# Keeping ScalarE's logarithm and exponential table loaded, and GLA's key·value products as three split fp32r passes

## The chip, the cores and the metric

The kernel runs on one core of one Trainium2 chip. The metric is the device time of one execution in microseconds, lower is better. A few executions are taken, and their median counts; one more execution is recorded by the profiler, and all rows below come from that one.

## The reference, cut to what matters

Two blocks work on 512 tokens of width 1024 in float32. The first block has two layers, one with latent attention, one with gated linear attention (GLA), each followed by a convolutional feed-forward layer. The second block runs differential attention beside a recurrent unit, gates the two branches, and ends in a mixture of 16 experts. The lines that the change touches:

```python
# GLA: 4 heads of 128 keys x 256 values, 8 chunks of 64 tokens
k_dec = k * jnp.exp(tot[:, :, None] - cum)
upd = jnp.einsum('bnchk,bnchv->nbhkv', k_dec, v)
def step(state, inp):
    g, u, qc = inp
    state = state * g[..., None] + u
    return state, jnp.einsum('bchk,bhkv->bchv', qc, state)
...
# second block
o = rms_norm_2(o, attn_subln_gain[l]) * (1.0 - lam_init)     # 8 heads
g_attn, g_lru = jnp.split(jax.nn.sigmoid(gate_pre + b_gates[l]), 2, axis=-1)
merged = g_attn * attn_d + g_lru * lru_d
x = x + jnp.einsum('bsd,de->bse', merged, w_out[l])
h2 = rms_norm_2(x, norm2_gain[l])
x = x + hierarchical_moe(h2, ...)                            # top 2 of one group of 4 experts
```

## The kernel before

All large products are made in a split form: an fp32 operand is divided into a high part (`ACT` copy into an fp32r tile, L286) and a low part (`DVE` subtract, L287), and `mm3` issues high·high, high·low and low·high (L309 to L311). Weights arrive by DMA on SP's queue as raw fp32 and are split in the same way by L94 (ACT) and L95 (DVE). PSUM has rings of banks, called "mm" for the linears and "at" for the rest.

**GLA** (`gla`). For each pair of heads the generator `recurrence` runs over eight chunks of 64 tokens beside the linears of the layer, one `step` between two pieces of a linear. `update(n)` multiplies the chunk's decayed keys, transposed (`kdt`, 64 tokens on the partitions by 128 keys), with the values (`v`, 64 tokens by 256 columns) for the two heads into one bank, L924: 32 such matmuls in all, in plain fp32. DVE adds the result to the running state (L929). L939 multiplies the queries with the state, also in fp32, one head into the upper and one into the lower 64 partitions of the result. `kdt` is a plain fp32 copy by DVE (L905 transposes), `v` one by ACT from the four banks of the value linear.

**Table loads.** ScalarE evaluates functions from a table set, and another set is brought in by an ACT_TABLE_LOAD. `rstd` (1/sqrt by exp of a logarithm) issues Ln at L366 and Exp at L367, and DVE finishes with a Newton step (L368 to L370). `log_exp_table` (L374) loads the set that holds both at a few places. Around rstd the kernel uses Tanh for gates (L1402, and L1454 for those kept "late") and Sqrt in the recurrent unit. A scheduler orders each engine's instructions; nothing but data ties Ln and Exp to the preload.

**Sub-norm stage** (second block, after attention). `sub_norm` brings eight heads back (L1279), squares (L1280), sums by PE, takes rstd, scales with DVE (L1284) and splits (L286, L287) into the inputs of the output linear. Gate linears (L1402) run beside it, and the late gates are held as plain sums until L1454 takes their Tanh.

**Routing stage** (`out_and_route`). For each of four token tiles and two halves: the residual is added (L1536), transposed by PE (L1539), squared by ACT (L1542), scaled (L1547 by DVE, L1549 by ACT) and multiplied with the router's weights (L1551). Then rstd over the row sums gives `route_rs` (L366, L367, L370). `route(t)` on DVE finds the two experts of a token (L1647 to L1663, result `sel`), PE counts positions from `sel` (L1667, L1668), and L1719 makes one-hot rows. After the fourth tile L1728 builds the lists by which POOL gathers the tokens of the first experts (L1758), PE transposes those (L1767), and the experts start. L1568 scales the rows that the gather reads.

Of the kernel before, what the change touches and what calls it, by code (L numbers as in the profile page):

```python
# [16 lines left out]
AF = mybir.ActivationFunctionType  # L17
# [4 lines left out]
P = 128  # L22
# [133 lines left out]
class Kern:  # L156
    def __init__(self, tc, ctx, a):
        self.tc, self.nc, self.a = tc, tc.nc, a
        self.n = 0
        self.cp = ctx.enter_context(tc.tile_pool(name="const", bufs=1))  # L160
        self.sp = ctx.enter_context(tc.tile_pool(name="small", bufs=4))
        mem = ctx.enter_context(tc.tile_pool(name="mem", bufs=1))
        psp = ctx.enter_context(tc.tile_pool(name="psum", bufs=1, space=PSUM))
        def new(n, dt, b):
            t = mem.tile([P, n], dt, tag=b, name=b)
            self.tags[id(t)] = b, n
            return t
        self.tags = {}
        self.rawq = deque(new(RAWN, F32, f"raw{i}") for i in range(3))
        self.wp = {"w": deque((new(PIECE, F32R, f"wh{i}"), new(PIECE, F32R, f"wl{i}")) for i in range(5))}  # L170
        self.pool = {F32: deque(), F32R: deque()}
        self.home, self.parts, self.held = {}, {}, set()
        self.bigs = {F32: [], F32R: []}
        quads = [(F32, new(RAWN, F32, f"f{i}"), 4) for i in range(5)]
        self.quads = [t for _, t, _ in quads]
        rquads = [(F32R, new(RAWN, F32R, f"rq{i}"), 4) for i in range(4)]
        self.rquads = [t for _, t, _ in rquads]
        ones = [(F32R, new(S, F32R, f"r{i}"), 1) for i in range(21)]
        bigs = [(dt, new(2 * S, dt, f"b{j}{i}"), 2) for j, dt in enumerate((F32, F32R)) for i in range(2)]

        self.side = None
        self.mem = mem
        for dt, t, k in quads + rquads + ones + bigs:
            parts = self.parts[id(t)] = [t[:, i * S:(i + 1) * S] for i in range(k)]
            if k == 2:
                self.bigs[dt].append(t)
            for x in parts:
                self.pool[dt].append(x)
                self.home[id(x)] = dt
        self.quad_parts = {id(x) for t in self.rquads for x in self.parts[id(t)]}  # L190
        self.banks = [psp.tile([P, S], F32, tag=f"ps{i}", name=f"ps{i}") for i in range(8)]
        self.rings(mm=4, at=4)
# [170 lines left out]

    def rstd(self, y, t, v, eps):
        nc = self.nc
        nc.scalar.activation(t, v, AF.Ln, bias=self.eps[eps])  # L366
        nc.scalar.activation(y, t, AF.Exp, scale=-0.5)  # L367
        nc.vector.scalar_tensor_tensor(t, y, -0.5, y, ALU.mult, ALU.mult)  # L368
        nc.vector.scalar_tensor_tensor(t, v, eps, t, ALU.add, ALU.mult)
        nc.vector.scalar_tensor_tensor(y, t, 1.5, y, ALU.add, ALU.mult)  # L370


    def log_exp_table(self):
        self.tc.keep_in_program_order(self.nc.scalar.preload_act_table_set("natural_log_exp_and_others"))  # L374


    def rstd_small(self, y, v):
# [466 lines left out]
    def gla(self, w, xh, xl, r_dram, after):  # L844
        nc, a = self.nc, self.a
        x = xh, xl
        self.rings(mm=5, at=3)
        wa2 = self.F()
        nc.scalar.dma_start(wa2[:32], a["w_a2"])
        at = self.F()  # L850
# [29 lines left out]
        q, kdt = [None] * 4, [None] * 4  # L880

        def ev(m, ps, t0, t1):
            p, j = divmod(m, 4)
            h = 2 * p + j % 2
            if j < 2:
                q[h] = self.F()
                nc.scalar.activation(q[h], ps, AF.Copy, scale=float(128 ** -0.5))
            else:

                nc.vector.tensor_tensor(kd[h], kd[h], ps, ALU.mult)  # L890
                ps = self.ps("at")
                for t in range(4):
                    nc.tensor.transpose(ps[:, t * P:t * P + P], kd[h][:, t * P:t * P + P], self.ident)
                kdt[h] = self.F()
                nc.vector.tensor_copy(kdt[h], ps)
                self.free(kd[h])

        on = [None] * 8
# [14 lines left out]
        def recurrence(p, v):  # L913
            st, oc = self.Fs(2), None
            on[4 * p:4 * p + 4] = self.Fs(4)
            late = None

            def update(n):
                t, p0 = n // 2, 64 * (n % 2)
                pu = self.ps("at")  # L920
                for i in range(2):
                    h = 2 * p + i
                    hs = slice(i * 256, i * 256 + 256)
                    nc.tensor.matmul(pu[:, hs], kdt[h][p0:p0 + 64, t * P:t * P + P], v[t][p0:p0 + 64, hs], start=True, stop=True)  # L924
                    cur, prev = (st[i][:, j * 256:j * 256 + 256] for j in (n % 2, 1 - n % 2))
                    if n == 0:
                        nc.vector.tensor_copy(cur, pu[:, hs])
                    else:
                        nc.vector.scalar_tensor_tensor(cur, prev, dec[h][:, n:n + 1], pu[:, hs], ALU.mult, ALU.add)  # L929
            update(0)  # L930
            yield
            for n in range(8):
                if n < 7:
                    update(n + 1)
                t = n // 2
                po = self.ps("at")[:, :256]

# [8 lines left out]
                if n % 2:  # L946
# [7 lines left out]
                    for i in range(2):  # L954
                        o = oc[:, i * 256:i * 256 + 256]
                        nc.vector.tensor_scalar(o, o, mv[:, i, 0:1], rs[:, i:i + 1], ALU.subtract, ALU.mult)
                    late = lambda t=t, oc=oc: turned(p, t, oc)
                yield
            self.free(st, v, q[2 * p:2 * p + 2], kdt[2 * p:2 * p + 2])
            late()  # L960

        def step():
            next(rec, None)

        def values(w, then):
            v, pss = self.Fs(4), [self.ps() for _ in range(4)]
            for i in range(4):
                z = next(w)
                then.prime(1) if i == 3 else w.prime(1)
                for t, ps in enumerate(pss):  # L970
                    ts = slice(t * P, t * P + P)
                    self.mm3(ps, [(xh[2 * i + k][:, ts], xl[2 * i + k][:, ts], *z(k)) for k in range(2)], i == 0, i == 3)
                    if i == 3:
                        nc.scalar.activation(v[t], ps, AF.Copy)
                z.done()
                step()
            return v
# [26 lines left out]
        ps = self.ps()[:32]  # L1004
# [315 lines left out]
    def lru_tile(self, m, px, pg, raw, y_dram):  # L1320
# [35 lines left out]
            nc.vector.scalar_tensor_tensor(u, u, 1.0, x, ALU.add, ALU.mult)  # L1356
            au.append((r, u, q))
        self.free(xh, xl, gh, gl)
        nc.scalar.activation(vv, vv, AF.Sqrt, scale=0.25)
        for d in range(2):  # L1360
            r, u, q = au[d]
            nc.vector.tensor_tensor(u, u, vv[:, d], ALU.mult)
# [34 lines left out]
    def gate(self, wg, i, h, ring="mm", then=None, late=False):  # L1397
        w = next(wg)
        (then or wg).prime(1)
        ps = self.mtile(w, KD, h, ring=ring)  # L1400
        t = self.F()
        self.nc.scalar.activation(t, ps, AF.Identity if late else AF.Tanh, bias=self.half_bg[:, i:i + 1], scale=0.5)  # L1402
        return t

    def second_norm(self, x, h, t0, t1):
# [3 lines left out]
    def second_block(self, x, h, o_dram, y_dram, g_dram):  # L1409
# [41 lines left out]
        for _ in norm:  # L1451
            pass
        for t in late.values():
            nc.scalar.activation(t, t, AF.Tanh)  # L1454
        self.free(h)


# [594 lines left out]
```

## Time and profile before

| what | value |
| --- | --- |
| runs | 2389.17, 2392.74, 2393.77 us (median 2392.74) |
| profiled execution | 2387.63 us, span 2385.7 us |
| PE, DVE, ACT busy | 98%, 70%, 55% of the span |
| mean granted TensorE clock | 0.99 |
| ACT_TABLE_LOADs | 56 of 1283 ns |

PE is the busiest engine nearly everywhere: of the span of 2385.7 us it has no work on it for 58.4 us. The granted clock is given as a share of 2.4 GHz, so 0.50 in a row is the 1.2 GHz level.

### The profile page before, as it was taken

To read this page: it belongs to the slowest core of one execution; us is meant where nothing else is said; L and a number is where in the kernel's file an instruction comes from. 1 tells how busy PE (TensorE), PEld (TensorE's weight loads), DVE (VectorE), ACT (ScalarE), POOL (GpSimd) and SP (SyncE) were. 2 spreads that over 40 slices of the span, in tenths; PEclk is the share of its full clock that TensorE was granted. 3 is DMA by queue.
4 is the path that set the end of the run, shared out by engine and by line. 5 is a ranking of instruction groups with operands and counts; after the bars stand their busy time and mean duration, and the time that the engine had idled before them with its cause. 6 is when DMAs were issued, how large, how long until landed. Compare 5 with 4: busy or idle time off the path is not lost.

```text
span 2385.7 us, 31840 instructions
## 1 busy us (share of the span) xinstructions
PE 2327.3 (98%) x12188; PEld 1963.4 (82%) x12188; DVE 1672.1 (70%) x3241; ACT 1301.5 (55%) x2053; POOL 82.1 (3%) x78
## 2 busy tenths in 40 slices
PE   8999999999999999999999999999999999799997
PEld 6888888888889776888888898888888778688886
DVE  7867678555558646585555578888888664699986
ACT  5444445333336424353333366777777843678886
POOL 0000000000000000000000000000000000012211
PEclk9999999999999999999999999999999999799999
DMA  4622211222232323222222323222322346499995
GB/s 172 208 73 83 102 58 71 107 91 104 90 114 69 124 80 102 84 88 107 91 104 90 114 73 122 89 93 72 124 71 98 115 163 252 153 353 395 389 391 179
DMA packets 66683, 325.32 MB, mean 136 GB/s; under 512 B 8256, under 2 KB 8896, under 8 KB 38112
## 3 DMA queue, kind: packets, MB, share of 16 engines
q1 hardware_dynamic: 50544, 281.83, 31.9%
q0 software_dynamic: 7584, 26.22, 3.8%
q10 hardware_dynamic: 8400, 15.21, 2.1%
q8 instruction: 97, 1.59, 0.3%
q14 instruction: 58, 0.48, 0.1%
HBM read 295.44 MB, written 27.79 MB: 135 GB/s over the span
## 4 chain that ended last, share of the span: by engine, by line
PE 74%; issue 9%; ACT 6%; DMA 5%; DVE 4%; POOL 1%; POOLq 0%; ACTq 0%; DVEq 0%
PE ps L309 22%; PE ps L310 22%; PE ps L311 22%; DMA out<-b,s 3%; PE ps L924 1%; PE ps L721 1%; ACT wh L94 1%; POOL out L1847 1%; PE ps L405 1%; PE ps L1234 0%; PE ps L1203 0%; ACT L366 0%; PE ps L1254 0%; ACT f L1239 0%; PE ps L939 0%
## 5 line engine op out<-in xcount | busy, mean ns | idle before, releaser
L94 ACT ACTIVATE wh<-raw 128x1024 fp32r<-128x1024 f32 (+2 forms) x374 | 383.4, 1030 | 527.7 <-PE ps L310 442.1
L95 DVE TENSOR_TENSOR wl<-raw,wh 128x1024 fp32r<-128x1024 f32 (+2 forms) x374 | 440.8, 1186 | 207.3 <-ACT wh L94 200.7
L310 PE MATMUL ps<-r,wh 128*128 128x512 f32 (+1 forms) x1308 | 485.0, 371 | 0.0
L309 PE MATMUL ps<-rq,wh 128*128 128x512 f32 (+1 forms) x1216 | 453.6, 375 | 12.6 <-ACT rq L286 9.9
L311 PE MATMUL ps<-rq,wl 128*128 128x512 f32 (+1 forms) x1216 | 450.3, 372 | 0.0
L309 PE MATMUL ps<-r,wh 128*128 128x512 f32 (+1 forms) x1160 | 421.0, 364 | 1.1 <-ACT r L433 0.8
L311 PE MATMUL ps<-r,wl 128*128 128x512 f32 (+1 forms) x1160 | 421.3, 364 | 0.7 <-DVE wl L95 0.7
L310 PE MATMUL ps<-rq,wh 128*128 128x512 f32 (+1 forms) x1032 | 372.7, 362 | 1.8 <-DVE rq L287 1.3
L311 PE MATMUL ps<-wh,r 128*128 128x512 f32 (+1 forms) x928 | 318.0, 343 | 0.4 <-DVE r L287 0.4
L310 PEld LDWEIGHTS ps<-r,wh 128*128 128x128 f32 x1308 | 246.3, 188 | 43.2 <-issue 3.1
L309 PEld LDWEIGHTS ps<-rq,wh 128*128 128x128 f32 x1216 | 229.6, 190 | 56.5 <-ACT rq L286 10.8
L311 PEld LDWEIGHTS ps<-rq,wl 128*128 128x128 f32 x1216 | 229.5, 189 | 38.6 <-issue 0.5
L309 PEld LDWEIGHTS ps<-r,wh 128*128 128x128 f32 x1160 | 218.7, 189 | 36.2 <-ACT r L433 1.5
L311 PEld LDWEIGHTS ps<-r,wl 128*128 128x128 f32 x1160 | 219.2, 189 | 35.0 <-DVE wl L95 1.0
L309 PE MATMUL ps<-wh,r 128*128 128x512 f32 (+1 forms) x640 | 238.7, 373 | 0.0
L310 PE MATMUL ps<-wl,r 128*128 128x512 f32 (+1 forms) x640 | 234.6, 367 | 0.0
L310 PEld LDWEIGHTS ps<-rq,wh 128*128 128x128 f32 x1032 | 195.8, 190 | 33.2 <-DVE rq L287 2.4
L311 PEld LDWEIGHTS ps<-wh,r 128*128 128x128 f32 x928 | 176.6, 190 | 21.3 <-DVE r L287 0.8
L309 PEld LDWEIGHTS ps<-wh,r 128*128 128x128 f32 x640 | 121.6, 190 | 18.3 <-issue 0.4
L310 PEld LDWEIGHTS ps<-wl,r 128*128 128x128 f32 x640 | 121.7, 190 | 17.9 <-issue 0.3
L310 PE MATMUL ps<-wl,rq 128*128 128x256 f32 (+1 forms) x320 | 95.3, 298 | 1.5 <-DVE wl L95 1.5
L309 PE MATMUL ps<-wh,rq 128*128 128x256 f32 (+1 forms) x320 | 96.4, 301 | 0.0
(653 smaller groups left out, 3512.3 us busy)
## 6 DMA issues: line engine op xcount, KB each, us to landing
raw<-w_ffn_up SPq DMA_DIRECT2D x44, 1024.0 KB, 4.8
f<-w_exp_in SPq DMA_DIRECT2D x21, 1024.0 KB, 9.7
raw<-w_exp_in SPq DMA_DIRECT2D x18, 1024.0 KB, 9.8
raw<-w_ffn_dn SPq DMA_DIRECT2D x16, 1024.0 KB, 4.8
raw<-w_exp_dn SPq DMA_DIRECT2D x9, 1024.0 KB, 10.4
f<-w_exp_dn SPq DMA_DIRECT2D x9, 1024.0 KB, 9.0
raw<-w_gla SPq DMA_DIRECT2D x17, 512.0 KB, 3.3
raw<-w_mla_o SPq DMA_DIRECT2D x8, 1024.0 KB, 4.9
```

What stands on the lines that cost most here:

```text
L94: k.nc.scalar.activation(h, src, AF.Copy)
L95: k.nc.vector.tensor_tensor(l, src, h.bitcast(F32), ALU.subtract)
L309: self.nc.tensor.matmul(out, ah, bh, start=f, stop=False)
L310: self.nc.tensor.matmul(out, ah, bl, start=False, stop=False)
L311: self.nc.tensor.matmul(out, al, bh, start=False, stop=e)
L405: nc.tensor.matmul(ps, ones, s[:, :n], start=i == group - 1, stop=i == len(tiles) - 1)
L721: self.nc.tensor.transpose(ps[:, o + (j - i) * P:o + (j - i + 1) * P], ea[j][:, i * P:(i + 1) * P], self.ident)
L924: nc.tensor.matmul(pu[:, hs], kdt[h][p0:p0 + 64, t * P:t * P + P], v[t][p0:p0 + 64, hs], start=True, stop=True)
L1847: self.nc.gpsimd.indirect_dma_start(out=out, out_offset=bass.IndirectOffsetOnAxis(ap=idx, axis=0), in_=y, in_offset=None, bounds_check=S - ...
```

## The change

Two edits that do not touch each other.

**Function tables.** Ln and Exp of `rstd` are queued behind the latest preload of the common table. The preload itself is queued behind the functions of other tables that were noted before it (`others`: Sqrt of the recurrent unit, Tanh of gates that are not late, late Tanh). The late Tanhs are queued behind all Exps of rstd that were noted (`exps`). All of these are orders within one engine's queue, without a semaphore. ACT_TABLE_LOADs in the program go from 56 to 41.

**Products.** `products(t)` handles two chunks at once: `kdt` and `v` are split into high and low fp32r tiles, and for each head the three passes are issued, each for the first chunk (rows 0 to 63, into one bank) and then the second (rows 64 to 127, into another). That makes 12 matmuls for each of 8 calls, 96 in all, for 32 fp32 ones. `kdt` and `v` go back with the last products. The rings of banks become 4 and 4, from 5 and 3.

```diff
     def rstd(self, y, t, v, eps):
         nc = self.nc
-        nc.scalar.activation(t, v, AF.Ln, bias=self.eps[eps])
-        nc.scalar.activation(y, t, AF.Exp, scale=-0.5)
+        ln = nc.scalar.activation(t, v, AF.Ln, bias=self.eps[eps]).ins
+        ex = nc.scalar.activation(y, t, AF.Exp, scale=-0.5).ins
+        for i in (ln, ex):
+            self.queue_behind(i, [self.table])
+        self.exps.append(ex)
...
     def log_exp_table(self):
-        self.tc.keep_in_program_order(self.nc.scalar.preload_act_table_set("natural_log_exp_and_others"))
+        self.table = self.tc.keep_in_program_order(self.nc.scalar.preload_act_table_set("natural_log_exp_and_others"))
+        self.table = getattr(self.table, "ins", self.table)
+        self.queue_behind(self.table, self.others)
+        self.others, self.exps = [], []
...
-        self.rings(mm=5, at=3)
+        self.rings(mm=4, at=4)
...
-                kdt[h] = self.F()
-                nc.vector.tensor_copy(kdt[h], ps)
+                kdt[h] = self.split_new(ps)
...
-            def update(n):
-                t, p0 = n // 2, 64 * (n % 2)
-                pu = self.ps("at")
+            def products(t):
+                pus = self.ps("at"), self.ps("at")
+                ts = slice(t * P, t * P + P)
+                for i in range(2):
+                    hs = slice(i * 256, i * 256 + 256)
+                    (kh, kl), (vh, vl) = kdt[2 * p + i], v[t]
+                    for j, (ka, vb) in enumerate(((kh, vh), (kh, vl), (kl, vh))):
+                        for c, pu in enumerate(pus):
+                            rows = slice(c * 64, c * 64 + 64)
+                            nc.tensor.matmul(pu[:, hs], ka[rows, ts], vb[rows, hs], start=j == 0, stop=j == 2)
+                if t == 3:
+                    self.free(v, kdt[2 * p:2 * p + 2])
+                return pus
+
+            def update(n, pu):
...
-                    nc.tensor.matmul(pu[:, hs], kdt[h][p0:p0 + 64, t * P:t * P + P], v[t][p0:p0 + 64, hs], start=True, stop=True)
...
-                        nc.scalar.activation(v[t], ps, AF.Copy)
+                        v[t] = self.split_new(ps)
...
         for t in late.values():
-            nc.scalar.activation(t, t, AF.Tanh)
+            i = nc.scalar.activation(t, t, AF.Tanh).ins
+            self.queue_behind(i, self.exps)
+            self.others.append(i)
```

The order of PE's instructions where the first products stand, before: L924 is the fp32 product, the L309 to L311 rows are the linear that runs beside it.

```order
L311 MATMUL ps_118<-r_90,wl_79 128x512
L924 MATMUL ps_119<-f_82,f_81 128x256
L309 MATMUL ps_114<-rq_88,wh_72 128x512
L310 MATMUL ps_114<-r_91,wh_72 128x512
L311 MATMUL ps_114<-rq_88,wl_73 128x512
L924 MATMUL ps_119<-f_82,f_80 128x256
L309 MATMUL ps_114<-rq_87,wh_72 128x512
```

And of the change, where L941 is the new product, L310 to L312 the linear's passes:

```order
L312 MATMUL ps_115<-r_90,wl_79 128x512
L941 MATMUL ps_120<-r_109,r_98 128x256
L941 MATMUL ps_121<-r_109,r_98 128x256
L941 MATMUL ps_120<-rq_86,r_98 128x256
L941 MATMUL ps_121<-rq_86,r_98 128x256
...
L941 MATMUL ps_121<-r_109,r_102 128x256
L310 MATMUL ps_116<-rq_88,wh_72 128x512
```

Each head's single product stood between pieces of the linear; now twelve stand in one run, alternating between two banks.

ScalarE's queue at the second token tile of the routing stage, before (L1542 square, L1549 scaling for the router, L1568 scaling for the gather):

```order
L1542 ACTIVATE b_111,route_ss<-b_110 128x512
L1549 ACTIVATE f_84<-ps_119,par 128x128
L366 ACT_TABLE_LOAD
L366 ACTIVATE s_15570<-s_15569,eps_175 128x1
L367 ACT_TABLE_LOAD
L367 ACTIVATE route_rs<-s_15570 128x1
L1549 ACTIVATE f_84<-ps_119,par 128x128
```

and of the change, with the same lines at new numbers (L1574 for L1542, L1581 for L1549, L367 and L368 for Ln and Exp):

```order
L1574 ACTIVATE b_111,route_ss<-f_83 128x512
L1581 ACTIVATE f_83<-ps_120,par 128x128
...
L1581 ACTIVATE f_84<-ps_119,par 128x128
L367 ACTIVATE s_15646<-s_15645,eps_175 128x1
L368 ACTIVATE route_rs<-s_15646 128x1
L1581 ACTIVATE f_84<-ps_119,par 128x128
```

The two loads of this tile are gone, as are those of the other three; the one preload stands ahead of the output linear.

ScalarE's queue at the end of the sub-norm stage, before (L1454 late Tanh, L286 split into the high part):

```order
L1454 ACTIVATE f_83<-f_83 128x512
L366 ACT_TABLE_LOAD
L366 ACTIVATE f_80<-ps_120,eps_175 128x512
L286 ACTIVATE r_100<-b_110 128x512
L367 ACT_TABLE_LOAD
L367 ACTIVATE f_84<-f_80 128x512
L366 ACT_TABLE_LOAD
L366 ACTIVATE f_83<-ps_121,eps_175 128x512
L1454 ACT_TABLE_LOAD
L1454 ACTIVATE f_81<-f_81 128x512
L367 ACTIVATE f_80<-f_83 128x512
```

and of the change (L1484 late Tanh, L287 split):

```order
L367 ACTIVATE f_84<-ps_121,eps_175 128x512
L1494 DMA f_82<-g_dram 128x512
L368 ACTIVATE f_84<-f_84 128x512
L1484 ACT_TABLE_LOAD
L1484 ACTIVATE f_82<-f_82 128x512
L287 ACTIVATE r_100<-b_110 128x512
L1484 ACTIVATE f_83<-f_83 128x512
L287 ACTIVATE rq_88<-f_81 128x512
L1484 ACTIVATE f_83<-f_83 128x512
L1484 ACTIVATE f_80<-f_80 128x512
L1484 ACTIVATE f_81<-f_81 128x512
...
L287 ACTIVATE rq_88<-f_81 128x512
```

Logarithms and exponentials now stand together ahead of one load and all eight late Tanhs; the splits of the last two heads stand among and behind these Tanhs.

## Rows read from the trace of the kernel before

**Rows 1.** The page: busy us, share of the span and instructions by engine.
```profile
PE 2327.3 (98%) x12188; PEld 1963.4 (82%) x12188; DVE 1672.1 (70%) x3241; ACT 1301.5 (55%) x2053; POOL 82.1 (3%) x78
```

**Rows 2.** Windows: span; PE, PEld, DVE, ACT, POOL busy (x); PEclk, DMA share, GB/s.
```profile
854.00:956.00 102.00, 102.00 (x437) 65.97 (x435) 59.11 (x173) 33.23 (x66) 0.00 (x0) 1.00 0.23 75
1850.00:1925.00 75.00, 71.70 (x327) 55.42 (x326) 51.76 (x89) 63.47 (x99) 1.08 (x2) 1.00 0.32 108
2100.00:2200.00 100.00, 100.00 (x507) 84.33 (x506) 91.22 (x96) 81.68 (x96) 21.01 (x11) 1.00 1.01 385
```

**Rows 3.** Timeline of PE, first products (each fp32 matmul is two records).
```profile
854.12 0.39 PE L311 MATMUL ps<-r,wl 128*128 128x512 f32 x1
854.43 0.70 PE L924 MATMUL ps<-f,f 64*128 64x256 f32 x2
855.06 0.50 PE L309 MATMUL ps<-rq,wh 128*128 128x512 f32 x1
855.39 0.39 PE L310 MATMUL ps<-r,wh 128*128 128x512 f32 x1
855.62 0.40 PE L311 MATMUL ps<-rq,wl 128*128 128x512 f32 x1
```

**Rows 4.** Timeline of PE: fp32r matmuls of 256 columns.
```profile
1012.03 0.28 PE L310 MATMUL ps<-r,wh 128*128 128x256 f32 x1
1012.15 0.28 PE L311 MATMUL ps<-r,wl 128*128 128x256 f32 x1
```

**Rows 5.** Timeline of PE: L939, one head alone, then two heads together.
```profile
869.90 0.65 PE L939 MATMUL ps<-f,f 128*64 128x256 f32 x2
870.48 0.66 PE L893 MATMUL ps<-ident,b 128*128 128x128 f32 x4
...
887.70 0.65 PE L939 MATMUL ps<-f,f 128*64 128x256 f32 x4
888.28 0.49 PE L309 MATMUL ps<-wh,rq 128*128 128x512 f32 x1
```

**Rows 6.** One line's instructions, L924: weight load's ns, minimum, median, maximum.
```profile
L924 PEld LDWEIGHTS ps<-f,f x28: 182/184/186, 854.4 to 954.2; 64*128 64x128 f32 x28
```

**Rows 7.** Timeline of ACT, routing stage, second token tile.
```profile
2036.74 1.28 ACT L366 ACT_TABLE_LOAD   x1
2038.03 0.29 ACT L366 ACTIVATE s<-s,eps 128x1 f32<-128x1 f32 x1
```

**Rows 8.** Chain that ended last, 2030 to 2080, shares by line.
```profile
by line: issue 31.2%; DMA b10p<-xs,s 11.7%; ACT L366 10.3%; ACT L367 10.0%; ACT wh L94 6.6%; DMA b11p<-xs,s 6.0%; PE ps L309 4.0%; PE ps L310 3.9%; PE ps L1551 3.6%; PE ps L311 3.5%; ACT f L1549 3.1%; ACT b L1542 2.9%; ACT s L366 2.4%; DVE 
```

**Rows 9.** Waits of PE, 2018 to 2080: us in total, times, longest.
```profile
PE ps L1668 <- DVE sel L1663: 6.4, 3, 3.4
PE ps L1551 <- ACT f L1549: 2.8, 2, 1.9
PE ps L1539 <- DVE f L1536: 1.4, 1, 1.4
PE ps L1539 <- DVE b L1536: 1.1, 2, 0.7
```

**Rows 10.** Timeline of PE, routing stage; idle time before, and its releaser.
```profile
2040.17 0.17 PE L1668 MATMUL ps<-sel,trib 128*128 128x16 bf16 x1 [2.23 <-DVE sel L1663]
```

**Rows 11.** One window of 5 us in the routing stage.
```profile
2040.00:2045.00 5.00, 4.83 (x18) 4.06 (x18) 3.65 (x24) 1.43 (x3) 0.00 (x0) 0.66 0.33 120
```

**Rows 12.** Waits of PE, 1850 to 1925.
```profile
PE ps L309 <- ACT rq L286: 1.6, 1, 1.6
PE ps L1234 <- ACT f L1239: 1.0, 1, 1.0
PE ps L310 <- DVE rq L287: 0.7, 1, 0.7
```

**Rows 13.** Timeline of ACT, end of the sub-norm stage: last Exp, last split.
```profile
1915.09 0.61 ACT L367 ACTIVATE f<-f 128x512 f32<-128x512 f32 x1
...
1920.30 0.63 ACT L286 ACTIVATE rq<-f 128x512 fp32r<-128x512 f32 x1 [3.14 <-DVE f L1284]
```

More of the change, by code (lines that the diff above doesn't have):

```diff
@@ L370, in rstd, with queue_behind @@
         nc.vector.scalar_tensor_tensor(y, t, 1.5, y, ALU.add, ALU.mult)
+    def queue_behind(self, ins, others):
+        for o in others:
+            self.tc.add_manual_dep(ins, o.name, mybir.DependencyInfo(mybir.DependencyClass.NoSync, mybir.DependencyReason.DATA),
+                                   reason="function table")
     def log_exp_table(self):
-        self.tc.keep_in_program_order(self.nc.scalar.preload_act_table_set("natural_log_exp_and_others"))
+        self.table = self.tc.keep_in_program_order(self.nc.scalar.preload_act_table_set("natural_log_exp_and_others"))
+        self.table = getattr(self.table, "ins", self.table)
+        self.queue_behind(self.table, self.others)
+        self.others, self.exps = [], []
     def rstd_small(self, y, v):
@@ L929, in update @@
                         nc.vector.scalar_tensor_tensor(cur, prev, dec[h][:, n:n + 1], pu[:, hs], ALU.mult, ALU.add)
-            update(0)
+            pus = products(0)
+            update(0, pus[0])
             yield
             for n in range(8):
+                if n % 2 and n < 7:
+                    pus = products(n // 2 + 1)
                 if n < 7:
-                    update(n + 1)
+                    update(n + 1, pus[(n + 1) % 2])
                 t = n // 2
@@ L958, in recurrence @@
                 yield
-            self.free(st, v, q[2 * p:2 * p + 2], kdt[2 * p:2 * p + 2])
+            self.free(st, q[2 * p:2 * p + 2])
             late()
@@ L965, in values @@
         def values(w, then):
-            v, pss = self.Fs(4), [self.ps() for _ in range(4)]
+            v, pss = [None] * 4, [self.ps() for _ in range(4)]
             for i in range(4):
@@ L1358, in lru_tile @@
         self.free(xh, xl, gh, gl)
-        nc.scalar.activation(vv, vv, AF.Sqrt, scale=0.25)
+        self.others.append(nc.scalar.activation(vv, vv, AF.Sqrt, scale=0.25).ins)
         for d in range(2):
@@ L1401, in gate @@
         t = self.F()
-        self.nc.scalar.activation(t, ps, AF.Identity if late else AF.Tanh, bias=self.half_bg[:, i:i + 1], scale=0.5)
+        ins = self.nc.scalar.activation(t, ps, AF.Identity if late else AF.Tanh, bias=self.half_bg[:, i:i + 1], scale=0.5).ins
+        if not late:
+            self.others.append(ins)
         return t
```

## Prediction

> **What bounds the kernel now.** I first read the busy times: PE has 2327.3 us of work recorded, DVE and ACT far less [rows 1]. So a microsecond is won in two ways only: less work on PE where PE is full, or less waiting of PE where it is not. Then I read windows around the places that the change touches [rows 2]. Around the GLA recurrence, 854 to 956 us, PE is busy for all 102.00 us, while ACT has 33.23 and DVE 59.11: there PE's work counts, and extra work on the other two does not. In the sub-norm stage PE lacks 3.3 us of 75, with ACT at 63.47: ACT is near its limit there. The list of PE's waits in the routing stage names selections, scaled activations and residual adds [rows 9], all of them links of one chain through ACT and DVE. The chain of waits over the same stretch confirms it: the table loads of L366 and L367 alone hold 10.3% and 10.0% of 50 us, that is 10.2 us [rows 8]. Behind it the expert stage has PE at 100.00 of 100 us [rows 2], so whatever is gained before it should carry to the end.
>
> **Products.** Removed: 32 fp32 matmuls. One takes 0.63 us from its start at 854.43 to the next start at 855.06, and it brings two small extras at its edges: the fp32r pass ahead of it takes 0.31 until the product starts, and the pass behind it 0.33, where a plain 512-column pass takes 0.23 [rows 3]. The body is 32 x 0.63 = 20.1 us.
>
> Added: 96 fp32r matmuls of 256 columns on 64 rows. The trace has none on 64 rows. The nearest row is 256 columns on 128 rows, 0.12 us from start to start [rows 4]; 96 x 0.12 = 11.5 us. The bounds: below, the two halves of the array might run side by side. L939 shows that this happens between column halves: one head alone takes 0.58 us to the next start, two heads together also 0.58 [rows 5]. Then a pair would take 0.12, and the sum would be 5.8 us. Above, the weight loads might not be hidden: a load of 64 rows takes 184 ns [rows 6], and with 0.11 of columns behind it each matmul would take 0.29, in all 27.8 us. I take 11.5: it is the row of the same type and width, and its loads are hidden.
>
> The edges: runs of fp32 work on PE fall from 32 to 15, counted in the two orders, since L924 now no longer breaks the linear. At about 0.08 us going in and 0.10 going out that is up to 3 us; the 8 new runs may pay the same for their own change, 1.4 us. I take 1.7. The term is 20.1 - 11.5 + 1.7 = **10.3 us**, with ends of -6.0 (loads exposed) and +16.0 (halves together).
>
> The splits of v and kdt add 12 instructions of 512 columns on ACT or DVE; such a split takes 0.63 us [rows 13]. PE has the linear to run meanwhile, and both engines have 40 us and more free in the window [rows 2]. If that cover were gone, a late v tile would cost its split, about 0.7 us, at the first product of each pair of heads, 1.4 us in all. Moving one bank from "mm" to "at" costs nothing as long as the first bank of the value linear is evacuated before the next linear begins; the value linear's last slices of the other three tiles (18 passes, about 4 us) lie between, and hide an evacuation of some 1.3 us.
>
> The Trainium skill, "TensorEngine Tiling (Array Packing)", Key Properties, has "Mode switching requires drain", for a change of mode and not of tile, and lets different tiles load and multiply in parallel. By that, alternating between two halves drains nothing inside a run of twelve, and the result would lie at the lower end, 5.8 us; the 16 changes of mode at the ends of runs are the edges counted above. The trace bears the parallel part out for column halves only [rows 5], and no row shows row halves in fp32r.
>
> **Tables, routing stage.** Eight loads go, two for each token tile. The load at 2036.74 is followed by its Ln at 2038.03, 1.29 us later [rows 7]; so a pair costs 2.57, and four pairs 10.3, all of them on the chain [rows 8]. But the first tile's pair lay beside full work of PE; of it only the next small wait can come back (0.4). That leaves 3 x 2.57 + 0.4 = 8.1. To this comes the clock: in 2040 to 2045 the granted clock was 0.66 [rows 11], a mix of both levels after PE had waited 2.23 us for a selection [rows 10]; that selection stood in DVE's queue behind a step that waited for the second tile's Exp. Without this wait the window's loss of 5 x (1 - 0.66) = 1.7 us goes too. So 9.8 at most. Against it stand the waits that PE has in the stretch: 6.4 + 2.8 + 1.4 + 1.1 = 11.7 us [rows 9], of which the last selection's 3.4 remains, since DVE computes it in an unbroken row after the last router matmul; 8.3 can go. The chain's other links (transposes, square, scaling, router, DVE's Newton step) stay, and keep some of this waiting. I take **8.5 us** with the clock in it, from 4 (half the waits return in another guise) to 10.
>
> The Trainium skill, "ScalarE: Activation LUTs", What ACT_TABLE_LOAD costs, gives 1283 ns for the load and about 1380 more of draining at every switch. By that eight loads would be worth 21 us on the chain; the row shows the function starting right behind the load [rows 7], so I go by the row.
>
> **Tables, sub-norm stage.** PE's waits are 1.6, 1.0 and 0.7 us, 3.3 in all [rows 12]. Before the last Exp at 1915.09 [rows 13] ACT's order has four loads close together, with late Tanhs between them. Without them (4 x 1.28, two Tanhs of 0.6) this Exp can come some 6 us earlier, near 1909. Now a load (1.28) and eight Tanhs stand behind it, with the last two splits among them, at about 0.6 us each by the rows of that size; so the last split ends near 1909.6 + 1.3 + 10 x 0.6 = 1917, where it ended at 1920.9 [rows 13]. PE, without its three waits, wants this split at about 1917.9. So the waits go, with a margin of some 0.9 us. I take **2.8 us**, from 0 to 3.3. The loads of late gates' partners from DRAM stand behind the Tanhs on ACT's queue; they are wanted 30 us later, behind the first output linear.
>
> Elsewhere (first block, attention) the positions of loads are unchanged, and I cost nothing.
>
> **Sum.** 10.3 + 8.5 + 2.8 = 21.6 us. From the profiled execution's 2387.63 that gives 2366.0. The median of the runs shown is 5.1 us above the profiled execution; against it the same sum gives 2371.1, and I predict **2371**.
>
> **Rivals.**
> 1. *Row halves run together.* For it: the column halves do [rows 5], and the two halves write different banks. Against: a stream of loads, one for each matmul, may set the pace whatever the halves do. GLA gives 16.0, the total 27.3: 2365.
> 2. *The routing waits return.* For it: the stage is one chain of many links, and the stores and the gather of rows follow it; a faster chain only meets the next link. Against: the loads are on the chain by name [rows 8]. Routing and sub-norm give 5 together: 2377.
> 3. *Loads of 64 rows are exposed*, 0.29 us a matmul. For it: L924's load of 184 ns is longer than the 0.12 that should hide it [rows 4, 6]. Against: the stream of rows 4 has a load for each of its matmuls too, and keeps 0.12 [rows 4]. GLA loses 6.0, and the tables' 11.3 leave 5.3: 2387, the edge of no change.
> 4. *Each change of row half empties the array* before the load begins: 0.29 and the 0.19 that an fp32 run's edges cost, 0.48 us a matmul, 46 us for 96. GLA loses 24, the tables give 11: 2406, slower. The point of decision is (20.1 + 1.7 + 11.3)/96 = 0.345 us a matmul; above it the whole change loses. For it: only that the edges of L924 cost something at all [rows 3]. Against: L939 changes its column half without a cost [rows 5].
> 5. *The experts are bound by their weights.* The share of DMA is 1.01 at 385 GB/s [rows 2], so an earlier start might only end in waiting for weights, and the tables' gain in the routing stage be lost: 2379. Against: PE is at 100.00 there with no wait for a weight, and the weights' queue itself waits for buffers to come free.
>
> **How the numbers follow.** A measurement of this kernel can tell about 0.2%, 4.8 us, from no change. Chances: the forecast 0.48, rival 1 0.20, rivals 2 and 5 together 0.18, rival 3 0.09, rival 4 0.05. Rival 3 lies on the bound and goes half to faster, half to the same; with 0.02 more for the runs' own spread of 4.6 us that makes faster 0.88, same 0.07, slower 0.05. The range reaches from below rival 1 to just short of rival 3, with the sub-norm's and routing's ends in it: 2361 to 2385.
>
> **What the profile after would show.** L941 at 0.12 us from start to start (0.06 for rival 1, 0.29 or more for 3 and 4), and a window around the recurrence some 10 us shorter. No table load between the squares and the gather; PE's wait for the second tile's selection gone, and the granted clock at 1.00 there; the gather some 8 us earlier against the start of the stage. In the sub-norm stage one load, eight Tanhs in a row, and PE without the waits for the last splits; if PE waits there for the last split behind the Tanhs, that step was wrong. The forecast fails as a whole if L941 takes more than about 0.35 us, or if PE waits on weights in the expert stage.

## The result, and the profile after

The changed kernel takes 2366.57 us (median of 4 runs, 2365.6 to 2369.79) where the kernel before took 2393.26 (4 runs, 2389.17 to 2394.19): a ratio of 0.9894, 95% interval 0.9877 to 0.9911, so 21 to 29 us faster. The forecast was 2371, from a sum of 21.6 us. The profiled executions are 2365.6 and 2387.63 us, 22.0 apart. This is inside the interval, and the profiled execution of the kernel before lies below all four of its runs, so the medians are further apart, 26.7 us.

The busy times of the changed kernel's page (us, share of the span, instructions) answer to [rows 1]:

```profile
span 2363.7 us, 31913 instructions
PE 2312.3 (98%) x12220; PEld 1959.9 (83%) x12220; DVE 1674.3 (71%) x3249; ACT 1285.0 (54%) x2042; POOL 82.1 (3%) x78
```

PE's busy time falls by 15.0 us, ACT's by 16.5. The traces hold 58 ACT_TABLE_LOADs before and 43 in the change, two more each than the 56 and 41 given ahead of the prediction; fifteen go either way, eight in the routing stage and seven in the sub-norm stage. To see where the 22 us came from I took the starts of seven PE instructions that every version has, from the PE timelines, and subtracted neighbours. They are, by the lines of the kernel before: the first L893 (transposes ahead of the first products, 843.29 us in the kernel before), the first L422 behind the recurrence (layer norm's sums, 1010.59), the last row of L422 (1402.49), the first L1203 (second block's attention, 1478.69), the first L1551 (router, 2014.37), the first L1767 (first gathered tokens, 2072.57), and the last record of PE (2372.41). All these stretches are in us:

| kernel | GLA | feed-forward | entry | attention to sub-norm and output | routing to gather | experts |
| --- | --- | --- | --- | --- | --- | --- |
| before | 167.30 | 391.90 | 76.20 | 535.68 | 58.20 | 299.84 |
| the change | 154.53 | 393.58 | 77.44 | 533.08 | 49.34 | 299.24 |
| products_only | 154.49 | 393.50 | 77.46 | 535.41 | 57.88 | 300.21 |
| tables_only | 167.29 | 391.91 | 76.01 | 531.72 | 49.84 | 299.34 |
| halves_in_sequence | 154.63 | 393.50 | 77.67 | 531.89 | 49.06 | 299.19 |
| same_rows | 158.30 | 393.51 | 75.88 | 533.46 | 50.08 | 299.84 |
| routing_loads_back | 154.55 | 393.51 | 77.54 | 534.84 | 57.89 | 300.21 |
| tanhs_free | 154.55 | 393.54 | 75.77 | 533.58 | 49.52 | 300.13 |
| rings_5_3 | 155.53 | 391.89 | 75.39 | 532.40 | 48.79 | 299.14 |
| sixteen_runs | 157.55 | 393.54 | 75.11 | 532.57 | 49.50 | 299.82 |
| rings_alone | 169.44 | 393.51 | 75.42 | 536.88 | 59.74 | 299.08 |
| rings_back | 154.67 | 391.89 | 76.20 | 531.72 | 49.09 | 299.46 |
| change_again | 154.51 | 393.49 | 77.53 | 531.94 | 49.49 | 299.41 |

The first two stretches repeat within 0.1 us between kernels that share the code there, far better than whole times, so they can be read where medians cannot. The stretch of attention and sub-norm varies by 1 to 2 us for one kernel (533.08 and 531.94 for the change). From before to the change: GLA gains 12.8, the feed-forward part loses 1.7, the entry of the second block loses 1.2, the sub-norm stretch gains 2.6, routing 8.9, the experts 0.6. The experts' part is within what other versions show (299.08 to 300.21). Together that is 21.9. Where a line's own time in the GLA stretch is given below, it is the sum from each of its starts to the next start on PE, from the same timelines.

The first run of products, PE's timeline of the change (answers to [rows 3]):

```profile
854.14 0.39 PE L312 MATMUL ps<-r,wl 128*128 128x512 f32 x1
854.46 0.38 PE L941 MATMUL ps<-r,r 64*128 64x256 f32 x2
854.68 0.28 PE L941 MATMUL ps<-rq,r 64*128 64x256 f32 x2
854.80 0.28 PE L941 MATMUL ps<-r,r 64*128 64x256 f32 x2
854.92 0.28 PE L941 MATMUL ps<-r,rq 64*128 64x256 f32 x2
855.04 0.28 PE L941 MATMUL ps<-rq,rq 64*128 64x256 f32 x2
855.15 0.28 PE L941 MATMUL ps<-r,r 64*128 64x256 f32 x2
855.36 0.50 PE L310 MATMUL ps<-rq,wh 128*128 128x512 f32 x1
855.70 0.40 PE L311 MATMUL ps<-r,wh 128*128 128x512 f32 x1
```

Each row is a pair, one matmul on each half of the rows, and pairs follow at 0.12 us. So two take what the forecast gave to one. The edges are still there: 0.32 us from the pass ahead until the first product, 0.22 for the first pair, 0.21 for the last, 0.34 behind it.

Not all products found a partner. The scheduler broke the eight calls into 12 runs on PE, and two of these hold six matmuls of one half alone; this is one of them:

```profile
904.89 0.50 PE L941 MATMUL ps<-r,r 64*128 64x256 f32 x2
905.23 0.63 PE L941 MATMUL ps<-r,rq 64*128 64x256 f32 x4
905.79 0.44 PE L917 MATMUL ps<-ident,f 128*128 128x128 f32 x2
```

Its six matmuls take 0.90 us, from 904.89 to 905.79, as long as the twelve from 854.46 to 855.36. Over the whole stretch, 37 pairs of the possible 48 start together and 22 matmuls start singly.

The routing stage's second tile on ACT, timeline of the change (answers to [rows 7]):

```profile
2023.70 0.28 ACT L367 ACTIVATE s<-s,eps 128x1 f32<-128x1 f32 x1
2024.02 0.20 ACT L368 ACTIVATE route_rs<-s 128x1 f32<-128x1 f32 x1
```

Ln and Exp follow at 0.32 us, where a load lay ahead of each. PE's waits from 2005 to 2070 (us in total, times, longest) answer to [rows 9]:

```profile
PE ps L1700 <- DVE sel L1695: 4.1, 3, 3.4
...
PE ps L1571 <- DVE f L1568: 0.8, 1, 0.8
...
PE ps L1571 <- DVE b L1568: 0.6, 1, 0.6
```

Of the 11.7 us before, 5.5 are left, and 3.4 of these are the last selection, as forecast; the waits for scaled activations (2.8) are gone. Between 2020 and 2025 us, where the second selection and its one-hot lie now, the granted clock stays at 1.00; it was 0.66 in [rows 11]. All four kernels with the eight loads (before, products_only, routing_loads_back, rings_alone) have a stretch of 3.4 to 6.8 us at the 1.2 GHz level ahead of the last selection; none of the nine without them has one.

```profile
2020.00:2025.00 5.00, 4.83 (x27) 3.73 (x27) 4.69 (x23) 1.97 (x7) 0.00 (x0) 1.00 0.33 129
```

In the sub-norm stage the three waits of [rows 12] are gone. This is the whole list of PE's waits from 1800 to 1940 in the change:

```profile
PE ps L1310 <- ACT f L1308: 0.6, 1, 0.6
```

### The profile page after: what moved, and what is told of

Its sections match the earlier page's. It is cut to its first block, busy times and chain, and to the rows that moved or that the text cites. A ratio compares the mean times of both kernels' runs of the same rounds, so it can differ in the third digit from the quotient of the medians.

```text
span 2363.7 us, 31913 instructions
## 1 busy us (share of the span) xinstructions
PE 2312.3 (98%) x12220; PEld 1959.9 (83%) x12220; DVE 1674.3 (71%) x3249; ACT 1285.0 (54%) x2042; POOL 82.1 (3%) x78
## 4 chain that ended last, share of the span: by engine, by line
PE 74%; issue 9%; DMA 5%; DVE 5%; ACT 5%; POOL 1%; POOLq 0%; SPq 0%; ACTq 0%; DVEq 0%
PE ps L310 22%; PE ps L311 22%; PE ps L312 22%; DMA out<-b,s 3%; PE ps L734 1%; POOL out L1879 1%; DVE wl L95 1%; DMA b11p<-xs,s 1%; PE ps L418 1%; DMA raw<-w_qk 1%; PE ps L1262 1%; PE ps L1263 0%; PE ps L1282 0%; PE ps L707 0%; ACT f L1267 0%
## 5 line engine op out<-in xcount | busy, mean ns | idle before, releaser
L311 PE MATMUL ps<-r,wh 128*128 128x512 f32 (+1 forms) x1296 | 482.1, 373 | 0.8 <-DVE r L447 0.7
L310 PE MATMUL ps<-rq,wh 128*128 128x512 f32 (+1 forms) x1204 | 450.3, 376 | 11.5 <-ACT rq L287 7.9
L312 PE MATMUL ps<-rq,wl 128*128 128x512 f32 (+1 forms) x1204 | 447.0, 372 | 0.0
L310 PE MATMUL ps<-r,wh 128*128 128x512 f32 (+1 forms) x1172 | 424.9, 364 | 1.3 <-ACT r L446 0.8
L312 PE MATMUL ps<-r,wl 128*128 128x512 f32 (+1 forms) x1172 | 424.0, 363 | 0.6 <-DVE wl L95 0.6
L311 PE MATMUL ps<-rq,wh 128*128 128x512 f32 (+1 forms) x1044 | 376.0, 361 | 1.1 <-DVE rq L288 0.6
L312 PE MATMUL ps<-wh,r 128*128 128x512 f32 (+1 forms) x928 | 318.0, 343 | 0.4 <-DVE r L288 0.4
L311 PEld LDWEIGHTS ps<-r,wh 128*128 128x128 f32 x1296 | 244.6, 189 | 42.5 <-DVE r L447 1.2
L310 PEld LDWEIGHTS ps<-rq,wh 128*128 128x128 f32 x1204 | 227.4, 190 | 54.7 <-ACT rq L287 8.3
L312 PEld LDWEIGHTS ps<-rq,wl 128*128 128x128 f32 x1204 | 227.3, 189 | 39.5 <-issue 1.2
L310 PEld LDWEIGHTS ps<-r,wh 128*128 128x128 f32 x1172 | 220.9, 189 | 36.4 <-ACT r L446 1.2
L312 PEld LDWEIGHTS ps<-r,wl 128*128 128x128 f32 x1172 | 221.2, 189 | 35.0 <-DVE wl L95 0.8
L310 PE MATMUL ps<-wh,r 128*128 128x512 f32 (+1 forms) x640 | 237.7, 371 | 0.0
L311 PE MATMUL ps<-wl,r 128*128 128x512 f32 (+1 forms) x640 | 234.0, 366 | 0.0
L311 PEld LDWEIGHTS ps<-rq,wh 128*128 128x128 f32 x1044 | 197.5, 190 | 31.7 <-DVE rq L447 1.2
L312 PEld LDWEIGHTS ps<-wh,r 128*128 128x128 f32 x928 | 176.4, 190 | 21.5 <-issue 1.2
L310 PEld LDWEIGHTS ps<-wh,r 128*128 128x128 f32 x640 | 121.1, 189 | 18.3 <-issue 0.4
L311 PEld LDWEIGHTS ps<-wl,r 128*128 128x128 f32 x640 | 121.0, 189 | 17.2
L311 PE MATMUL ps<-wl,rq 128*128 128x256 f32 (+1 forms) x320 | 95.4, 298 | 1.4 <-DVE wl L95 1.4
L310 PE MATMUL ps<-wh,rq 128*128 128x256 f32 (+1 forms) x320 | 96.6, 302 | 0.0
## 6 DMA issues: line engine op xcount, KB each, us to landing
f<-w_exp_in SPq DMA_DIRECT2D x21, 1024.0 KB, 10.2
```

The costliest lines, as they stand in the source:

```text
L310: self.nc.tensor.matmul(out, ah, bh, start=f, stop=False)
L311: self.nc.tensor.matmul(out, ah, bl, start=False, stop=False)
L312: self.nc.tensor.matmul(out, al, bh, start=False, stop=e)
```

## The experiments

**Each edit alone.** First the products without the orders among functions, with Ln, Exp, preloads and Tanhs free as before:

```diff
     def queue_behind(self, ins, others):
-        for o in others:
+        for o in ():
```

> The split products alone; Ln, Exp, preloads and Tanhs are left unordered as before the change. If the two edits add up, this run has the whole shift of the GLA stage (12.7 us at the end of the recurrence in the changed kernel's trace) and gives about 3 us of it back before 1480 us: 2393 - 10 = 2383 us. If what was given back there is chance of that execution and no consequence of the earlier arrival, 2380. If the products only pay together with the tables, above 2388.

Measured: 2379.06 us (6 runs) against 2389.7 (11 runs), ratio 0.9952, interval 0.9938 to 0.9966, 8 to 15 us faster. By stretches it has the change's GLA (154.49), feed-forward (393.50) and entry (77.46), and the rest is that of the kernel before (535.41, 57.88).

Then the orders alone, with `gla` of the kernel before put back whole:

```diff
-        self.rings(mm=4, at=4)
+        self.rings(mm=5, at=3)
...
-                kdt[h] = self.split_new(ps)
+                kdt[h] = self.F()
+                nc.vector.tensor_copy(kdt[h], ps)
...
-            def products(t):
...
+            def update(n):
```

> The orders of the function tables alone; GLA as before, with its fp32 products and rings of 5 and 3. If the edits add up: 2.6 us in the sub-norm stage and 9.4 in routing, 2393 - 12 = 2381 us. By the price of a load with a drain behind it (2.66 us each, eight on the chain) the routing alone would give 21: 2370.

Measured: 2376.9 us (6 runs), ratio 0.9945, interval 0.9933 to 0.9957, 10 to 16 us faster; GLA 167.29 as before, routing 49.84 as in the change. So the edits add up: 10.6 and 12.8 us of the medians make 23.4, within the interval of the whole. The price with a drain behind each load (2370) is out.

**The routing loads back.** The preload no longer stands behind functions of other tables:

```diff
-        self.queue_behind(self.table, self.others)
```

> The whole change, but the preload is no longer queued behind the functions of other tables, so that it stands too early for the routing stage and the eight loads of Ln and Exp return there; the sub-norm stage keeps its one load and its Tanhs at the end. If the routing stage gained 9.4 us by these loads: 2366.6 + 9 = 2376 us, and PE's waits for selections and scaled activations come back. If the gain there came from elsewhere (the order of DVE or PE), less than 4: under 2371.

Measured: 2375.25 us (6 runs), ratio 0.9933, interval 0.992 to 0.9945. The routing stretch is 57.89, so 8.6 us of the 8.9 hang on these eight loads, 1.07 each. That is what a load is worth to the stage and not its own length, since the granted clock falls again with the loads, to 0.72 from 2030 to 2035 us. And the waits of [rows 9] are back in PE's list:

```profile
PE ps L1699 <- DVE sel L1694: 6.4, 3, 3.4
...
PE ps L1582 <- ACT b L1580: 2.3, 1, 2.3
PE ps L1570 <- DVE f L1567: 1.8, 2, 1.4
PE ps L1582 <- ACT f L1580: 0.9, 1, 0.9
```

The edit touched the sub-norm stage too, though its one load and its order of Tanhs stayed. The stretch is 534.84 us, above all eight kernels with every order kept (531.72 to 533.46), and the list of PE's waits from 1800 to 1940 has two where the change has one of 0.6 us:

```profile
PE ps L1309 <- ACT f L1307: 1.8, 1, 1.8
PE ps L1261 <- ACT f L1291: 0.8, 1, 0.8
```

So the place of the preload is part of what the sub-norm stage gained. This rests on one profiled execution.

**Tanhs not behind the Exps.**

```diff
-            self.queue_behind(i, self.exps)
```

> The whole change, but the late Tanhs are not queued behind the Exps, so two or three loads return in the sub-norm stage; routing stays without loads. If the sub-norm stage's 2.6 us come from its loads, one to two of them go: 2367.5 to 2369. If that gain came from the earlier preload and the splits' order, no change within 0.5 us in the stage's own shift.

Measured: 2365.13 us (4 runs), ratio 0.99, interval 0.9882 to 0.9917. The stretch is 533.58, half a microsecond above the change's first profile and 1.6 above its second, though L367 and L368 have one load more each. Inconclusive for the size: an expected loss of 1 to 2 us stands beside a spread of 1.7 us among the eight kernels with every order kept (531.72 to 533.46). One of the three waits of [rows 12], for a low part, is back in the list from 1800 to 1940:

```profile
PE ps L1310 <- ACT f L1308: 0.7, 1, 0.7
PE ps L311 <- DVE rq L288: 0.7, 1, 0.7
```

The three kernels without any order have 535.41 to 536.88 us, so this one execution keeps 1.8 to 3.3 us of the gain without the order of the Tanhs. That most of the gain comes from elsewhere is likely by it, and not shown.

**Do the row halves run side by side?** Both chunks' products read rows 0 to 63, so the second chunk's products are made of the wrong tokens:

```diff
-                            rows = slice(c * 64, c * 64 + 64)
+                            rows = slice(0, 64)
```

> The whole change, but both chunks' products read rows 0 to 63 (so the second chunk's products are made from the first chunk's tokens; same count, sizes and banks). If the pairs of L941 start together because they lie on different halves of the array, here they must follow one another at 0.12 us: L941 takes about 5 to 6 us more, 15 to 16 us for 96 in place of 9.7, and the time rises to about 2371 to 2372. If the halves have nothing to do with it, L941 and the time stay.

Measured: 2367.74 us (4 runs), ratio 0.9907, interval 0.989 to 0.9923. The medians can't place it, but the trace can. The first run of products, timeline of PE:

```profile
854.49 0.50 PE L941 MATMUL ps<-r,r 64*128 64x256 f32 x2
854.83 0.39 PE L941 MATMUL ps<-rq,r 64*128 64x256 f32 x2
855.07 0.40 PE L941 MATMUL ps<-r,r 64*128 64x256 f32 x2
855.30 0.40 PE L941 MATMUL ps<-r,rq 64*128 64x256 f32 x2
```

Pairs now follow at 0.24, one matmul behind the other. L941 takes 13.69 us here and 9.72 in the change. The stretch is 3.8 us longer (158.30 against 154.53), not the 5 to 6 expected: 48 x 0.12 = 5.8 would be saved if every pair started together, and in the change only 37 do. So running side by side is shown, and it is worth 3.8 us here.

**Does the order of the halves matter?** In each group the three passes of one half, then the three of the other:

```diff
-                    for j, (ka, vb) in enumerate(((kh, vh), (kh, vl), (kl, vh))):
-                        for c, pu in enumerate(pus):
+                    for c, pu in enumerate(pus):
+                        for j, (ka, vb) in enumerate(((kh, vh), (kh, vl), (kl, vh))):
```

> The whole change, but in each group of six products the three passes of the first chunk (rows 0 to 63) come first and the three of the second behind them, so that neighbours are mostly on the same rows. If two row halves run side by side only when neighbours lie on different halves, a group of twelve loses up to 0.06 us for each of two thirds of its matmuls: L941 goes from 0.10 to about 0.14 us a matmul, the time 3 to 6 us up, 2370 to 2373. If the pace is set by weight loads or by columns whatever the rows, L941 and the time stay: 2366.6.

Measured: 2364.3 us (4 runs), ratio 0.9888, interval 0.9873 to 0.9904; L941 9.97 us, GLA 154.63. The expected loss is not there, and the reason is not the other theory either. The timeline of PE shows pairs all the same:

```profile
856.46 0.39 PE L941 MATMUL ps<-r,r 64*128 64x256 f32 x2
856.68 0.29 PE L941 MATMUL ps<-rq,r 64*128 64x256 f32 x2
856.80 0.29 PE L941 MATMUL ps<-r,r 64*128 64x256 f32 x2
856.92 0.28 PE L941 MATMUL ps<-r,rq 64*128 64x256 f32 x2
```

In PE's queue the first half's passes stand as r,r, then rq,r, then r,r, and the second half's same three behind them; the scheduler has kept that order. In the trace each starts beside its like of the other half. So the second half did not wait for the first half's three passes.

**What a run of products costs at its edges.** Each pair's products issued head by head at two steps, 16 runs in place of 12. In this kernel some of their banks are overwritten by other results before they are read, which changes the values and not the counts.

```diff
+                if n % 2 == 0 and n < 6:
+                    nxt = self.ps("at"), self.ps("at")
+                    products(n // 2 + 1, nxt, (0,))
```

> The whole change, but each pair's products are issued head by head at two steps of the recurrence, so that the 96 matmuls stand in 16 runs on PE instead of 12. If what L941 takes above 48 x 0.12 = 5.8 us (3.9 us) is the price of entering and leaving runs, L941 and the linear's passes next to it take about 1 to 2 us more here (0.3 a run). If it is spread over the matmuls, nothing changes.

Measured: 2367.54 us (4 runs), ratio 0.9911, interval 0.9895 to 0.9928; GLA 157.55, 3.0 us more. L941 takes 10.20 us (+0.5), the linear's passes 131.18 (+1.2), and the queries' products 11.31 (+1.7), since the pairs of heads there are broken too. The part that was expected, L941 and the linear, is 1.6 us for four runs, 0.4 each.

**The banks.** The change with the rings of 5 and 3 kept:

```diff
-        self.rings(mm=4, at=4)
+        self.rings(mm=5, at=3)
```

> The whole change with the rings of 5 and 3 banks kept as before. If the prediction's step was right that the bank moved costs nothing, and three banks are enough for two of products and one of outputs, the stage's shift stays at 12.7 us within 0.5. If three banks make the products wait for the state's updates, PE shows waits for DVE in the recurrence and the stage loses 1 to 4 us.

Measured: 2365.59 us (4 runs), ratio 0.9904, interval 0.9887 to 0.9921. GLA is 155.53, one microsecond more, with 14 runs of products in place of 12 and no new wait on DVE to speak of (0.2). The surprise stands in the next column: the feed-forward stretch is 391.89, as in the kernel before, where every kernel with rings of 4 and 4 has 393.5. The rings that `gla` sets stay in force behind it. Two kernels test that: the kernel before with rings of 4 and 4 and nothing else,

```diff
     def gla(self, w, xh, xl, r_dram, after):
-        self.rings(mm=5, at=3)
+        self.rings(mm=4, at=4)
```

> The kernel before with rings of 4 and 4 banks in GLA and in all that follows up to the second block, and nothing else of the change. If the rings cost what is lost behind the recurrence, the stretch from there to the end of the second feed-forward layer takes 455.9 us in place of 454.1, and the time is 1.7 us up, which the times alone can hardly tell. If the loss belongs to the products, 454.1.

and the change with the rings of 5 and 3 set again behind the last linear beside the recurrence:

```diff
         self.linear(w, 8, KD, x, ev_r, then=wo)
+        self.rings(mm=5, at=3)
```

> The whole change, and behind the last linear that runs beside the recurrence the rings of 5 and 3 banks are set again, as the kernel before has them there. If the 1.8 us that every version with rings of 4 and 4 loses between the recurrence and the end of the second feed-forward layer (454.1 to 455.9 us) come from these rings, that stretch returns to about 454.2 while the GLA stretch stays at 154.5: the best time so far, 2 us under the change. If they come from arriving earlier or from the split tiles, it stays at 455.9.

The change ran beside them:

> The change itself beside these two on one chip, for the comparison: 2366.6 us by the first result, and 154.5 and 455.9 us in the two stretches.

Measured against 2390.33 (15 runs): rings_alone 2393.82 (11 runs), ratio 1.0016, interval 1.0007 to 1.0025; rings_back 2363.57 (4 runs), 0.9896, 0.9881 to 0.9911; change_again 2364.36 (4 runs), 0.9897, 0.9881 to 0.9912. Feed-forward: 393.51, 391.89 and 393.49 us. The loss goes with the rings, with or without the products, and goes away with them. With the old products rings of 4 and 4 also cost 2.1 us inside GLA (169.44), which nobody had asked. PE's waits in the layer norm, first of the change (1000 to 1040), then of rings_back (from the longer list of 985 to 1460), show part of what is lost:

```profile
PE ps L311 <- DVE r L447: 0.7, 1, 0.7
PE ps L312 <- DVE wl L95: 0.6, 1, 0.6
PE ps L310 <- ACT r L446: 0.3, 1, 0.3
PE ps L310 <- DVE s L774: 0.2, 1, 0.2
```

```profile
PE ps L312 <- DVE wl L95: 0.7, 1, 0.7
...
PE ps L310 <- ACT r L446: 0.3, 1, 0.3
```

The wait for a low part (L447) and the one for DVE's statistics (L774) are only there with four banks in "mm"; they make 0.9 of 1.6 us. The rest is spread over PE's passes there and was not traced further. rings_back and rings_5_3 have the shortest sums of stretches (1503.0 and 1503.1 us, against 1507.2 and 1506.4 of the change's two profiles), but the median of rings_back is only 0.8 us under that of change_again, and the runs of the two overlap.

## Why the prediction came out, step by step

**The time.** The sum of 21.6 us was worked out for the profiled execution, and the two profiled executions are 22.0 apart. Of the 4.5 us between 2371 and 2366.57, 4.1 come from the step from there to the medians: the forecast put 5.1 us between profiled execution and median, and the change's median is only 1.0 above its own. The medians differ by 26.7 us here and by 26.0 beside change_again; with one profile of the kernel before, the record does not show where the 4 us beyond the stretches' sum lie. That the sum came so near is in part luck: GLA gave 2.5 us more than forecast, and 1.7 and 1.2 us that nobody forecast were lost behind it.

**Products: 10.3 us forecast; GLA gave 12.8, and 1.7 were lost behind it.** Summed from start to start over the stretch, L924 took 18.92 us and L941 takes 9.72: 9.2, where the forecast had 20.1 - 11.5 = 8.6. The step that failed is the price of 0.12 us *a matmul*: rival 1 was right that the halves run together, at 0.12 a pair. But the body is not then 5.8 us. The prediction counted eight new runs with every matmul paired, and the trace has 12 runs with 37 pairs and 22 single matmuls: 59 x 0.117 = 6.9 us, and 2.8 for the edges of the products themselves, 0.2 at each run (first start 0.22, last 0.21, as above) and some more where a run is broken off. So the mechanism of rival 1 happened without its price, 16.0. The edges elsewhere were mis-sized the other way: 1.7 was taken, and the linear's passes fell from 131.91 to 130.03, the queries' products from 10.90 to 9.58 and the transposes by 0.4, 3.6 us in all. What was not seen is the queries' part: with the products out of the way both heads stand together, and [rows 5] had the price of that already.

**"Moving one bank costs nothing" failed.** The reason given holds inside GLA, where 4 and 4 are better by 1.0 with the new products. But the ring stays so through the layer norm and the second feed-forward layer and costs 1.6 us there, shown by rings_alone and rings_back.

**A rival at the entry of the second block that I had not named.** There the change lost 1.2 us. The window of its trace has the granted clock at 0.76, that of tanhs_free, whose program is the same up to there, at 1.00:

```profile
1455.00:1460.00 5.00, 4.01 (x13) 3.12 (x14) 5.00 (x15) 2.51 (x7) 0.54 (x1) 0.76 0.71 252
```

```profile
1455.00:1460.00 5.00, 3.58 (x16) 2.88 (x17) 5.00 (x16) 2.77 (x7) 0.54 (x1) 1.00 0.72 272
```

Five of the ten profiled executions with the products have this dip (77.4 to 77.7 in the table's entry column), the others and those without the products have 75.1 to 76.2. It follows a wait of PE for a split, 1.8 us long in the change and 1.7 in tanhs_free, which has no dip. Up to there tanhs_free has the same program as the change, change_again, products_only and routing_loads_back, which all have the dip; so the code alone does not decide it. The length of the wait does not either: it is 1.8 to 2.2 us in the five with the dip, but 2.1 in rings_back and 2.2 in the kernel before, which have none. Whether the edit makes the dip more likely stays open, since none of the three kernels without the products has it.

**Routing: 8.5 forecast, 8.9 measured**, 8.6 of it shown to hang on the loads. That the chain of waits put the loads at 10.2 us was a good upper bound, and the reason for staying below it held: the last selection still takes 3.4 us of waiting.

**Sub-norm: 2.8 forecast, 2.6 between the two profiles**, and up to 4.0 with other executions of the same code. The three waits of [rows 12] are gone and one of 0.6 us is new, which makes 2.7. The last split comes in time, but not by the step that the prediction has: it counted the Tanhs as what holds this split up. In the change the eighth Tanh ends at 1903.68, and ACT then waits for DVE's scaling:

```profile
1902.54 1.14 ACT L1484 ACTIVATE f<-f 128x512 f32<-128x512 f32 x2
1905.85 0.63 ACT L287 ACTIVATE rq<-f 128x512 fp32r<-128x512 f32 x1 [2.18 <-DVE f L1312]
```

The split ends at 1906.48. The second block's attention starts 9.8 us earlier than in the kernel before (1468.87 against 1478.69), so counted in that kernel's times it is 1916.3, near the forecast's 1917 through another chain, the one through DVE. That near hit is luck. That the Tanhs' own order matters was not shown.

**Rivals.** The routing waits did not return (2), the loads of 64 rows are hidden (3), a change of row half costs nothing inside a run (4), and the experts kept all of the earlier start (5): that stretch is 299.24 against 299.84. The Trainium skill, "TensorEngine Tiling (Array Packing)", Key Properties, was right that tiles work in parallel, and its drain at a change of mode agrees with edges of 0.2 us at each run in the products and 0.4 with the linear beside them, though no run separates a drain from other causes. The Trainium skill, "ScalarE: Activation LUTs", What ACT_TABLE_LOAD costs, has a drain of some 1380 ns beside the load. The trace does not show one: behind the Ln of [rows 7], which ends at 2038.32 in the kernel before, the load for Exp starts at 2038.34, and Exp at 2039.64, 0.02 us behind the load's end.

```profile
2038.34 1.28 ACT L367 ACT_TABLE_LOAD   x1
2039.64 0.20 ACT L367 ACTIVATE route_rs<-s 128x1 f32<-128x1 f32 x1
```

The 8.6 us of the eight loads fit that: they are less than eight times 1.28.

## What to carry to other kernels

Small matmuls on 64 rows are best counted in pairs and in runs: two on different halves take the time of one, if the scheduler leaves both in one run, and each time PE leaves the long stream for them costs some tenths of a microsecond on both sides, also for whatever else stood between. An order among functions of one table is worth the loads that lie on the chain of waits there, and that chain gives an upper bound before the change is made (10.2 us here, for 8.6). A setting like the number of banks in a ring holds until it is set again, so look for its price behind the stage that it was made for.

## What the runs showed of the hardware

- Matmuls on rows 0 to 63 and on rows 64 to 127, with weight loads of their own, start together: pairs at 0.12 us, against 0.24 when both are on the same rows.
- They do so even when three passes of one half stand ahead of those of the other in the program: the trace shows the halves' passes starting in pairs again (L941 9.97 us against 9.72).
- Five of the ten executions with the products were at 1.2 GHz for 3.4 us after the same wait of PE at the second block's entry. Of five with the same code up to there four had it and one had not; the entry took 77.4 to 77.7 us with it and 75.1 to 76.2 without.
- In the second token tile's rows of the kernel before, a table load starts 0.02 us behind the function ahead of it, takes 1.28 us, and the next function starts 0.02 us behind its end.
